# Low parts of the down-projection weights: a negated copy on ScalarE and an adding transfer in place of a subtraction on VectorE

## The chip, the cores and the metric

The kernel runs on one core of one Trainium2 chip. The metric is the device time of one execution in microseconds (us). The kernel before was timed in three runs, and the median stands for it.

## The reference, cut to what matters

One decoder layer on 256 tokens of width 2048, in float32: a mixer (a gated recurrence and a differential attention, side by side), a layer norm, a SwiGLU network, a second layer norm, a gate with a per-layer input, and a third layer norm. The change touches the third product of the SwiGLU network alone, the one with `w_down` (5632 x 2048):

```python
def swiglu(h, w_gate, w_up, w_down):
    g = jnp.einsum('bsd,df->bsf', h, w_gate)
    u = jnp.einsum('bsd,df->bsf', h, w_up)
    return jnp.einsum('bsf,fd->bsd', jax.nn.silu(g) * u, w_down)

h = layer_norm(ALPHA * h + swiglu(h, w_gate, w_up, w_down), ln2_g, ln2_b)
```

## The kernel before, in words

**The split.** Every large product is made from high and low parts: a float32 value is written as hi + lo = w, where hi is the value rounded to the type `fp32r` of the tensor engine and lo is what remains. A product is then three matmuls (hi x hi, hi x lo, lo x hi). The activations are split once per stage; the weights are split as they arrive.

**The weight stream.** All weights are cut into units of 128 x 2048 float32 (1 MB each). The class `Stream` holds them in the order of their use. A unit is loaded on the SyncE queue (SP) into a buffer `w`, of which there are three (line 96). It is then split by halves of 128 x 1024: ScalarE (ACT) writes the high part `wh` (line 114, `prepare_hi`), and VectorE (DVE) subtracts it from the loaded weights and writes the low part `wl` (line 106, `prepare_lo`). There are six buffers for `wh` and six for `wl`, so six halves can be under way.

**The order.** The tensor engine's work is cut into quarters of a unit. After each, `tick()` emits the stages of all other work that are due and then calls `prepare()`: the low part of the half whose high part was emitted last, the loads that have become possible, and the high part of one more half if there is room for it (`room`: at most six halves ahead of those given back). Each engine runs what was emitted for it in that order:

```python
def prepare(self):
    if self.los < self.his:
        self.prepare_lo()
    self.load()
    if self.room():
        self.prepare_hi()
```

**The SwiGLU network.** The hidden width is walked in three parts (`FPARTS`) of 16, 16 and 12 tiles of 128 features. Each part first makes its gate and up products (lines 196 and 197), then its down product: four column blocks of 512, each from 4, 4 or 3 units of `w_down` (16, 16 and 12 units, 44 in all, 88 halves). `token_rows` makes for each row tile and each half of the tokens three matmuls of 512 columns (lines 222 to 224); line 223 is the only one that reads `wl`. A half of a unit is used by 12 such matmuls:

```python
nc.tensor.matmul(ps, ah, wh[:, c], start=first, stop=False)
nc.tensor.matmul(ps, ah, wl[:, c], start=False, stop=False)
nc.tensor.matmul(ps, al, wh[:, c], start=False, stop=last)
```

In the last block of the last part, the last two units are walked twice, for one half of the tokens after the other (`token_halves`), and the second layer norm starts between the two.

**GpSimd (POOL)** issues a few loads of its own (the residual input, norm weights, biases) and does small arithmetic of the norms (lines 621 to 623). It issues nothing while the down products run, up to the norm that ends the third part.

Of the kernel before, what the change touches and what calls it, by code (L numbers as in the profile page):

```python
# [11 lines left out]
F32 = mybir.dt.float32  # L12
# [39 lines left out]
class Stream:  # L52
    """The weight units [128, 2048] in the order of their use, and the work that runs
    beside them. The tensor engine's work is cut into quarters of a unit; after each,
    tick() emits a stage of every job that is due, and then prepares weights: a unit is
    loaded, and split by halves, hi + lo = w exactly, each with at most 12 significant
    bits."""

    def __init__(self, nc, pool, srcs, after_load, pairs):
        self.nc, self.pool, self.srcs, self.after_load = nc, pool, srcs, after_load  # L60
        self.order = [(n, j) for n in range(len(srcs)) for j in range(2)]
        for n in pairs:
            self.order[2 * n:2 * n + 4] = [(n, 0), (n + 1, 0), (n, 1), (n + 1, 1)]
        self.loaded = self.released = self.his = self.los = 0
        self.freed = self.seen = 0
        self.w32, self.parts, self.jobs, self.spare = {}, {}, [], []
        self.unit = 0
        self.held = False
# [35 lines left out]
    def prepare_lo(self):  # L104
        wh, wl = self.parts[self.order[self.los]]
        self.nc.vector.tensor_tensor(wl, self.source(self.los), wh.bitcast(F32), ALU.subtract)  # L106
        self.released += self.order[self.los][1]
        self.los += 1
        self.load()

    def prepare_hi(self):
        src = self.source(self.his)
        wh, wl = self.new_half()
        self.nc.scalar.copy(wh, src)  # L114

# [41 lines left out]
def tile_hybrid_layer(ctx: ExitStack, tc: tile.TileContext, t: dict):  # L157
# [8 lines left out]
    # ---------------------------------------------------------------- the weight units  # L166
# [8 lines left out]
    pair = len(srcs)  # L175
    for f0, nf in FPARTS:
        srcs += [t[n][f0 + i] for i in range(nf) for n in ("w_gate", "w_up")]
        srcs += [t["w_down"][f0 // 4 + kq, blk] for blk in range(4) for kq in range(nf // 4)]
    srcs += [t["w_pg"][blk, kq] for blk in range(4) for kq in range(4)]
    after_load = {}  # L180
    st = Stream(nc, wp, srcs, after_load, [pair])
# [7 lines left out]
    # ---------------------------------------------------------------- products  # L189
    def feature_rows(ps, n, xhl, k0, k1):  # L190
        """ps [128 features, tokens] += unit n's row tiles k0..k1 times x: x_hi W_hi + x_hi W_lo
        in the first half of the bank, x_lo W_hi in the second."""
        for k in range(k0, k1):
            wh, wl = st.half(n, k // 8)
            c = slice((k % 8) * P, (k % 8 + 1) * P)
            nc.tensor.matmul(ps, wh[:, c], xhl[:, k, :], start=(k == 0), stop=False)  # L196
            nc.tensor.matmul(ps[:, :S], wl[:, c], xhl[:, k, :S], start=False, stop=(k == KT - 1))  # L197

    def feature_major(xhl, name, units=1):
        """The next units, row tiles outside."""  # L200
        n = st.take(units)
        pss = [bank(name) for _ in range(units)]
        for q in range(4):
            for u, ps in enumerate(pss):
                feature_rows(ps, n + u, xhl, 4 * q, 4 * q + 4)
                st.free(q % 2)
                st.tick()
        return pss if units > 1 else pss[0]

    def gather(out, ps):  # L210
        """out = the sum of both halves of a feature-major bank, in two stages."""
        nc.scalar.copy(out, ps[:, S:])  # L212
        yield
        nc.vector.tensor_tensor(out, ps[:, :S], out, ALU.add)

    def token_rows(ps, n, ahl, i, k, h, first, last, cols=slice(0, 512)):
        """ps [tokens of half h, columns] += a's row tile k times row tile i of unit n."""
        wh, wl = st.half(n, i // 2)
        c = slice((i % 2) * 512 + cols.start, (i % 2) * 512 + cols.stop)
        ah = ahl[:, k, h * P:(h + 1) * P]  # L220
        al = ahl[:, k, S + h * P:S + (h + 1) * P]
        nc.tensor.matmul(ps, ah, wh[:, c], start=first, stop=False)  # L222
        nc.tensor.matmul(ps, ah, wl[:, c], start=False, stop=False)  # L223
        nc.tensor.matmul(ps, al, wh[:, c], start=False, stop=last)  # L224

    def token_major(ps, ahl, kq, first, last):
        """ps[half] += a's row tiles of quarter kq times the next unit."""
        n = st.take()
        for i in range(4):
            for h in range(2):  # L230
                token_rows(ps[h], n, ahl, i, 4 * kq + i, h, first and i == 0, last and i == 3)
            st.free(i % 2)
            st.tick()

    def token_halves(ps, ahl, kqs, first, last, then=None):
        """The next units, one token half after the other."""
# [14 lines left out]
    # ---------------------------------------------------------------- start  # L251
# [3 lines left out]
    # the tensor engine's clock rises while the first loads are on their way  # L255
# [20 lines left out]
    # x^T, split: [:, k, :256] high parts, [:, k, 256:] low parts; it comes in along  # L276
    # with the first weight units, which take it as it comes
# [44 lines left out]
    # ---------------------------------------------------------------- small values  # L322
# [7 lines left out]
    def small_values():  # L330
        # softplus(-lambda) = max(-lambda, 0) + log1p(e), e = exp(-|lambda|);
        # log1p(e) = 2 atanh(e / (2 + e)) by its series, e / (2 + e) <= 1/3
# [8 lines left out]
        # lambda of the differential attention, on every partition  # L341
# [26 lines left out]
    def relative_bias():  # L368
        # r[h, j] = table[bucket(255 - j), h], masked where 255 - j < 0, on 128 rows
        rps = aux("rps")  # L370
        nc.tensor.matmul(rps[:H, :RW], rb, oh, start=True, stop=True)
        yield
        nc.vector.tensor_copy(rv[:, :S], rps[:H, :S])
        nc.vector.memset(rv[:, S:], NEG)
        nc.gpsimd.dma_start(rd1, rv)
        nc.gpsimd.dma_start(rd, rd1.unsqueeze(1).broadcast_to([H, P, RW]))

    # ---------------------------------------------------------------- RG-LRU
    # 128 channels at a time: convolution and gates
# [40 lines left out]
    def recurrence():  # L420
        # a = exp(-8 gate softplus); with t = tanh(4 gate softplus) = (1 - a) / (1 + a),
        # sqrt(1 - a^2) = (1 + a) sqrt(t)
# [24 lines left out]
    # values, token-major  # L447
# [8 lines left out]
    for blk in range(2):  # L456
        ps = [bank("vps") for _ in range(2)]
        for kq in range(4):
# [3 lines left out]
            if blk == 1 and kq == 0:  # L462
                # bt[p, h, c] = r[h, 127 - p + c] (columns 0..127: the block below the diagonal
                # one, 128..255: the diagonal block): rows of r, read with a pitch one short
# [4 lines left out]
    # ---------------------------------------------------------------- heads  # L469
    mhl = act.tile([P, KT, 2 * S], F32R, tag="A", name="mhl")  # L470

    def lru_out(b, ps):
        """y gelu(yg), split, as row tile b of the merged heads."""
# [25 lines left out]
    def attention(h, qps, kps):  # L499
# [11 lines left out]
        # the two score heads on the diagonal of [2 * 64, 2 * keys]  # L511
# [7 lines left out]
        # scores; softmax_1 - lambda softmax_2 of the head, [queries, keys] by blocks  # L519
# [39 lines left out]
        # times values; RMS norm, [queries, features] by blocks  # L559
# [34 lines left out]
    # ---------------------------------------------------------------- output projection, LN1  # L594
# [22 lines left out]
    def norm_scale(stats, h, n=4):  # L617
        """mean, 1 / deviation, - mean / deviation"""
# [32 lines left out]
    def norm_to(script, xhl, pss, scale, stats, gb, cols):  # L651
        """z <- LN(z); xhl <- z^T, split, in the order of the script: by ticks, the steps of
        token half h and column block b: sh the last residual and the scale, uhb and zhb the
        norm, thb the transposition and high part, lhb the low part; vhb keeps a block of the
        per-layer inputs; H and L prepare weights.
        A block with xhb is scaled before the transposition, thb, takes g and b after it, yhb,
        and rhb does the same for z."""
# [73 lines left out]
    def ple_unit():  # L731
        """Half of the per-layer input projection."""
# [19 lines left out]
    # the projection of the per-layer input runs while the norm is worked out  # L752
# [3 lines left out]
    # ---------------------------------------------------------------- SwiGLU, LN2  # L756
# [41 lines left out]
    # ---------------------------------------------------------------- per-layer gate, LN3  # L798
# [36 lines left out]
    # the last block: the second token half's columns in two pieces, one after the other  # L835
# [47 lines left out]
def _buckets():  # L883
    """T5 bucket of each distance 0..255 (a constant of the shapes)."""
# [18 lines left out]
def _stationary(w):  # L903
    """(2048, F) -> (F/128, 128 rows, 16 row tiles * 128 features)."""
# [4 lines left out]
def _moving(w):  # L909
    """(R, C) -> (C/512, R/512, 128 rows, 4 row tiles * 512 columns)."""  # L910
# [4 lines left out]
def _channels(a):  # L915
    """(..., 1024) -> (128, 8, ...)"""
# [49 lines left out]
```

## Time and profile before

| what | value |
|---|---|
| median of three runs | 1204.46 us (1200.2 to 1206.15) |
| the profiled execution: span from the first to the last instruction | 1199.7 us |
| TensorE busy (PE) | 1182.0 us, 99% of the span |
| VectorE busy (DVE) | 775.7 us, 65% |
| ScalarE busy (ACT) | 607.5 us, 51% |
| GpSimd busy (POOL) | 34.3 us, 3% |
| bytes moved by DMA | 234.83 MB, 196 GB/s over the span |

For the profiled execution only its span is given; what lies around the span is not shown by itself. The median of the runs is 4.8 us longer than that span. Times are in microseconds from the start of the span; MB are millions of bytes, so a unit of "1024.0 KB" is 1.049 MB. Matmuls are pipelined, and one that is shown as 0.39 us long is followed by the next after about 0.23 us.

### The profile page before, as it was taken

Reading aid. Unit: us, or ns where it says so; the run is one execution under the profiler, and the core shown is the slowest. Engines: PE = TensorE matmul, PEld = TensorE weight load, DVE = VectorE, ACT = ScalarE, POOL = GpSimd, SP = SyncE. Lnnn points to the kernel's source line nnn. Section 1 sums busy time; section 2 is a strip of 40 time slices with the busy share of each in tenths; the row PEclk is TensorE's granted clock in tenths of the full one; section 3 lists DMA queues with packets and bytes.
Section 4 is the critical chain, followed back from the end, with each engine's and each line's share of the span. In section 5 each row is a group of like instructions: output and inputs, shape, how many; then the busy total and the mean of one; then the engine's idle time right before and its main releaser. Section 6 shows DMA issues by size and latency. Waiting matters only on the chain.

```text
span 1199.7 us, 15640 instructions
## 1 busy us (share of the span) xinstructions
PE 1182.0 (99%) x6210; PEld 1008.2 (84%) x6210; DVE 775.7 (65%) x1066; ACT 607.5 (51%) x945; POOL 34.3 (3%) x60
## 2 busy tenths in 40 slices
PE   9999999999999999999999999999999999999995
PEld 7888888888888888888888888888888888887885
DVE  6976988785678555564455555554455555556977
ACT  6767576664456454443335444443344454435640
POOL 0000000001010000000000000000000000002001
PEclk9999999999999999999999999999999999999998
DMA  9765454547638555555555555555555555554741
GB/s 332 263 219 196 174 176 148 181 164 287 235 119 315 183 203 177 200 186 197 189 199 187 176 189 196 176 181 205 186 200 176 190 196 175 182 204 150 281 166 70
DMA packets 38872, 234.83 MB, mean 196 GB/s; under 512 B 4432, under 2 KB 8440, under 8 KB 12048
## 3 DMA queue, kind: packets, MB, share of 16 engines
q1 hardware_dynamic: 35952, 221.51, 52.7%
q0 software_dynamic: 2848, 12.34, 2.7%
q8 instruction: 48, 0.79, 0.2%
q14 instruction: 24, 0.20, 0.0%
HBM read 231.72 MB, written 3.68 MB: 196 GB/s over the span
## 4 chain that ended last, share of the span: by engine, by line
PE 94%; DVE 3%; ACT 1%; POOL 1%; DMA 1%; issue 0%; SPq 0%; DVEq 0%; POOLq 0%; ACTq 0%
PE u L196 13%; PE g L196 13%; PE u L197 7%; PE g L197 7%; PE dps L223 7%; PE dps L224 7%; PE dps L222 6%; PE ops L222 2%; PE ops L223 2%; PE ops L224 2%; PE xr L196 2%; PE k L196 2%; PE yg L196 2%; PE q L196 2%; PE gps L223 2%; PE gps L222 2%
## 5 line engine op out<-in xcount | busy, mean ns | idle before, releaser
L106 DVE TENSOR_TENSOR wl<-w,wh 128x1024 fp32r<-128x1024 f32 x404 | 493.0, 1223 | 277.3 <-ACT wh L114 271.3
L114 ACT CAST wh<-w 128x1024 fp32r<-128x1024 f32 x404 | 423.9, 1052 | 309.3 <-PE dps L224 143.7
L196 PE MATMUL u<-x,wh 128*128 128x512 f32 x688 | 243.4, 396 | 0.0
L196 PE MATMUL g<-x,wh 128*128 128x512 f32 x688 | 243.4, 396 | 0.0
L197 PE MATMUL u<-x,wl 128*128 128x256 f32 x688 | 193.0, 281 | 0.0
L197 PE MATMUL g<-x,wl 128*128 128x256 f32 x688 | 193.0, 281 | 0.0
L196 PEld LDWEIGHTS u<-x,wh 128*128 128x128 f32 x688 | 129.1, 188 | 30.8
L196 PEld LDWEIGHTS g<-x,wh 128*128 128x128 f32 x688 | 129.1, 188 | 30.8
L222 PE MATMUL dps<-wh,hT 128*128 128x512 f32 x352 | 137.1, 389 | 0.0
L224 PE MATMUL dps<-wh,hT 128*128 128x512 f32 x352 | 137.0, 389 | 0.0
L223 PE MATMUL dps<-wl,hT 128*128 128x512 f32 x352 | 137.0, 389 | 0.0
L197 PEld LDWEIGHTS g<-x,wl 128*128 128x128 f32 x688 | 130.0, 189 | 0.1
L197 PEld LDWEIGHTS u<-x,wl 128*128 128x128 f32 x688 | 130.0, 189 | 0.0
L222 PEld LDWEIGHTS dps<-wh,hT 128*128 128x128 f32 x352 | 66.1, 188 | 13.8
L223 PEld LDWEIGHTS dps<-wl,hT 128*128 128x128 f32 x352 | 66.1, 188 | 13.6
L224 PEld LDWEIGHTS dps<-wh,hT 128*128 128x128 f32 x352 | 66.1, 188 | 13.6
L212 ACT COPY g<-g 128x256 f32<-128x256 f32 x43 | 16.0, 372 | 79.4 <-PE g L197 79.4
L212 ACT COPY uu<-u 128x256 f32<-128x256 f32 x43 | 16.0, 373 | 77.0 <-PE u L197 77.0
L222 PE MATMUL ops<-wh,mhl 128*128 128x512 f32 x128 | 50.3, 393 | 0.0
L223 PE MATMUL ops<-wl,mhl 128*128 128x512 f32 x128 | 49.9, 390 | 0.0
L224 PE MATMUL ops<-wh,mhl 128*128 128x512 f32 x128 | 49.9, 390 | 0.0
L196 PE MATMUL xr<-xhl,wh 128*128 128x512 f32 x128 | 46.5, 406 | 1.6 <-ACT wh L71 1.5
(227 smaller groups left out, 1598.6 us busy)
## 6 DMA issues: line engine op xcount, KB each, us to landing
w<-in_w_gate SPq DMA_DIRECT2D x44, 1024.0 KB, 4.9
w<-in_w_up SPq DMA_DIRECT2D x44, 1024.0 KB, 4.8
w<-in_w_down SPq DMA_DIRECT2D x44, 1024.0 KB, 4.9
w<-in_w_a SPq DMA_DIRECT2D x28, 1024.0 KB, 4.9
w<-in_w_out SPq DMA_DIRECT2D x16, 1024.0 KB, 4.9
w<-in_w_pg SPq DMA_DIRECT2D x16, 1024.0 KB, 5.0
w<-in_w_v SPq DMA_DIRECT2D x8, 1024.0 KB, 4.9
lng<-in_ln_g POOLq DMA_DIRECT2D x3, 1024.0 KB, 5.9
```

The costliest lines, as they stand in the source:

```text
L106: self.nc.vector.tensor_tensor(wl, self.source(self.los), wh.bitcast(F32), ALU.subtract)
L114: self.nc.scalar.copy(wh, src)
L196: nc.tensor.matmul(ps, wh[:, c], xhl[:, k, :], start=(k == 0), stop=False)
L197: nc.tensor.matmul(ps[:, :S], wl[:, c], xhl[:, k, :S], start=False, stop=(k == KT - 1))
L212: nc.scalar.copy(out, ps[:, S:])
L222: nc.tensor.matmul(ps, ah, wh[:, c], start=first, stop=False)
L223: nc.tensor.matmul(ps, ah, wl[:, c], start=False, stop=False)
L224: nc.tensor.matmul(ps, al, wh[:, c], start=False, stop=last)
```

## The change

For the units of `w_down` alone (their numbers are collected in the set `by_dma`), the subtraction on DVE is left out. In its place ACT, right after the high part, writes the negated high part into `wl`, and a transfer issued on the GpSimd queue reads the same half of the weights from memory a second time and adds it to what stands in `wl`. The unit's load into `w` stays, since the high part is made from it. All other weights keep the old way. (The diff also blanks comments.)

```diff
     def prepare_lo(self):
         wh, wl = self.parts[self.order[self.los]]
-        self.nc.vector.tensor_tensor(wl, self.source(self.los), wh.bitcast(F32), ALU.subtract)
+        if self.order[self.los][0] not in self.by_dma:
+            self.nc.vector.tensor_tensor(wl, self.source(self.los), wh.bitcast(F32), ALU.subtract)
         self.released += self.order[self.los][1]
         self.los += 1
         self.load()

     def prepare_hi(self):
         src = self.source(self.his)
+        n, j = self.order[self.his]
         wh, wl = self.new_half()
         self.nc.scalar.copy(wh, src)
+        if n in self.by_dma:
+            self.nc.scalar.mul(wl, wh.bitcast(F32), -1.0)
+            self.nc.gpsimd.dma_start(wl, self.srcs[n][:, j * 1024:j * 1024 + 1024], accum_op=ALU.add)
...
+    by_dma = set()
     for f0, nf in FPARTS:
         srcs += [t[n][f0 + i] for i in range(nf) for n in ("w_gate", "w_up")]
+        by_dma.update(range(len(srcs), len(srcs) + nf))
         srcs += [t["w_down"][f0 // 4 + kq, blk] for blk in range(4) for kq in range(nf // 4)]
```

## Rows read from the trace of the kernel before

**Rows 1.** The page, busy time of each engine and share of the span.

```profile
span 1199.7 us, 15640 instructions
PE 1182.0 (99%) x6210; PEld 1008.2 (84%) x6210; DVE 775.7 (65%) x1066; ACT 607.5 (51%) x945; POOL 34.3 (3%) x60
```

**Rows 2.** Waits of PE, whole span: total us, times, longest.

```profile
PE tp L681 <- ACT z L675: 1.6, 2, 1.4
PE xr L196 <- ACT wh L71: 1.5, 1, 1.5
PE wps L260 <- DVE zero L257: 1.2, 1, 1.2
PE sps L526 <- DVE khl L517: 0.6, 1, 0.6
```

**Rows 3.** Waits in the first down stage (537 to 626), all engines.

```profile
ACT wh L114 <- PE dps L224: 52.7, 32, 1.7
DVE wl L106 <- ACT wh L114: 42.5, 32, 1.5
```

**Rows 4.** Timeline of PE at the first down stage's start and end (start, length).

```profile
536.99 0.39 PE L222 MATMUL dps<-wh,hT 128*128 128x512 f32 x1
...
623.84 0.39 PE L224 MATMUL dps<-wh,hT 128*128 128x512 f32 x1
624.07 0.39 PE L196 MATMUL g<-x,wh 128*128 128x512 f32 x1
```

**Rows 5.** Timeline of ACT around the first down stage's start (start, length).

```profile
523.25 1.05 ACT L114 CAST wh<-w 128x1024 fp32r<-128x1024 f32 x1 [1.00 <-ACT g L764]
...
537.46 1.05 ACT L114 CAST wh<-w 128x1024 fp32r<-128x1024 f32 x1
...
539.99 1.05 ACT L114 CAST wh<-w 128x1024 fp32r<-128x1024 f32 x1 [1.07 <-PE dps L224]
542.72 1.05 ACT L114 CAST wh<-w 128x1024 fp32r<-128x1024 f32 x1 [1.68 <-PE dps L224]
```

**Rows 6.** The page, costliest groups: both halves of the split (busy, mean ns, idle before).

```profile
L106 DVE TENSOR_TENSOR wl<-w,wh 128x1024 fp32r<-128x1024 f32 x404 | 493.0, 1223 | 277.3 <-ACT wh L114 271.3
L114 ACT CAST wh<-w 128x1024 fp32r<-128x1024 f32 x404 | 423.9, 1052 | 309.3 <-PE dps L224 143.7
```

**Rows 7.** Groups of ACT by form, whole span: scaled and plain passes of one size.

```profile
L764 ACT ACTIVATE g<-g 128x256 f32<-128x256 f32 x44 | 18.5, 420 | 0.4 <-DVE g L214 0.4
L770 ACT CAST hT<-g 128x256 fp32r<-128x256 f32 x44 | 17.9, 407 | 1.0 <-DVE g L768 0.9
L684 ACT CAST x<-tp 128x512 fp32r<-128x512 f32 x10 | 5.8, 588 | 2.6 <-PE tp L681 2.6
L675 ACT ACTIVATE z<-z,mv 128x512 f32<-128x512 f32 x6 | 4.9, 817 | 4.6 <-POOL mv L623 4.6
```

**Rows 8.** Stretches: busy of PE, PEld, DVE, ACT, POOL; clock, DMA share, GB/s.

```profile
523.00:537.00 14.00, 6.51 (x9) 1.00 0.57 187
537.00:626.00 89.00, 89.00 (x397) 73.77 (x396) 45.81 (x44) 35.46 (x35) 0.00 (x0) 1.00 0.56 195
```

(The first of the two was asked for ACT alone.)

**Rows 9.** The same view, two stretches with transfers of both queues under way.

```profile
372.00:380.00 8.00, 8.00 (x49) 7.06 (x48) 4.36 (x6) 5.05 (x8) 0.00 (x0) 1.00 1.01 425
292.00:300.00 8.00, 8.00 (x37) 6.64 (x36) 5.99 (x8) 3.17 (x3) 0.00 (x0) 1.00 1.02 421
```

**Rows 10.** Groups of POOL: issue of its transfers (busy, mean ns, idle before).

```profile
L605 POOL DMA_DIRECT2D z<-in_x x4 | 3.0, 742 | 5.6 <-PE ups L578 5.6
L805 POOL DMA_DIRECT2D pb<-in_b_ple x4 | 2.2, 562 | 23.7 <-DVE pg L812 23.7
```

**Rows 11.** DMA view, 65 to 79: GB/s in 40 slices; issue with KB, us to landing.

```profile
GB/s 140 164 351 398 492 304 328 468 191 247 211 211 212 211 211 211 211 211 211 211 211 234 374 211 328 418 439 376 464 373 347 240 279 328 174 224 402 424 421 398
...
rd<-rd POOLq DMA_DIRECT2D x1, 1536.0 KB, 13.7
```

**Rows 12.** DMA view, 280 to 300: issues, KB each, us to landing.

```profile
w<-in_w_out SPq DMA_DIRECT2D x4, 1024.0 KB, 8.5
z<-in_x POOLq DMA_DIRECT2D x4, 512.0 KB, 8.6
```

**Rows 13.** Timeline of SP around the first down stage (start, from first to last, issues).

```profile
523.21 71.09 SPq L96 DMA_DIRECT2D w<-in_w_down  x14
599.41 0.33 SPq L96 DMA_DIRECT2D w<-in_w_gate  x1
```

**Rows 14.** Stretches in which PE pauses (columns as in the second of rows 8).

```profile
6.00:10.00 4.00, 2.54 (x13) 1.80 (x12) 2.36 (x7) 2.23 (x7) 0.00 (x0) 1.00 0.97 295
1090.00:1095.00 5.00, 3.62 (x20) 2.65 (x19) 2.83 (x4) 2.21 (x4) 3.33 (x4) 1.00 0.10 30
1190.00:1199.70 9.70, 0.00 (x0) 0.00 (x0) 5.60 (x9) 0.00 (x0) 2.44 (x3) 0.50 0.28 108
```

**Rows 15.** The page, bytes read and written in memory.

```profile
HBM read 231.72 MB, written 3.68 MB: 196 GB/s over the span
```

More of the change, by code (lines that the diff above doesn't have):

```diff
@@ L52, with __init__ @@
 class Stream:
-    def __init__(self, nc, pool, srcs, after_load, pairs):
+    def __init__(self, nc, pool, srcs, after_load, pairs, by_dma):
+        self.by_dma = by_dma
         self.nc, self.pool, self.srcs, self.after_load = nc, pool, srcs, after_load
@@ L180, in tile_hybrid_layer @@
     after_load = {}
-    st = Stream(nc, wp, srcs, after_load, [pair])
+    st = Stream(nc, wp, srcs, after_load, [pair], by_dma)
     def bank(name):
```

## The prediction, made before the changed kernel was run

> **What bounds the kernel now.** I read the busy times first, then the waits of PE, then the down stage by itself. PE is busy for 1182.0 of 1199.7 us [rows 1], and its own waits add up to under 5 us, none of them on a low part `wl` [rows 2]. So PE's sequence of matmuls sets the time, and work taken off another engine is worth only what PE waits for it.
>
> In the first down stage the waits run the other way: ACT waits 32 times for PE to give a `wh` buffer back, and DVE 32 times for ACT [rows 3]. Both preparing engines are ahead of PE; the subtraction that the change removes ends early each time. PE walks the 16 units from 536.99 to 624.07 [rows 4], 87.08 us: 5.44 us for a unit, 2.72 us for a half. ACT copies a half every 2.73 us [rows 5], so the whole chain runs in step with PE.
>
> How far ahead is it? The copy at 539.99 was released by the end of the first half's matmuls and fills its buffer for the seventh half (six buffers). The first half's copy is therefore six copies earlier, at 523.25 [rows 5], 13.7 us before PE uses it at 536.99 [rows 4]. That lead is all that a slower way of making `wl` can use up.
>
> **The change, part by part.**
>
> *DVE.* 88 subtractions of 1.223 us go [rows 6]: 108 us of DVE time, 1.2 us out of each 2.72. Gain: nothing, as DVE is ahead [rows 2, 3].
>
> *ACT.* 88 negations are added. A plain pass over 1024 columns takes 1.052 us [rows 6]. A scaled pass was 1.03 times a plain one at 256 columns and 1.39 times at 512 (there with two per-row operands) [rows 7], so 1.05 to 1.46 us. I take 1.06, as the change's scale is a constant. ACT then needs 2.1 us (at most 2.5) of each 2.72; before the stage, where swiglu work runs beside it, it was busy 6.51 of 14 us [rows 8], and five negations make that 11.8. It stays inside: cost nothing, and what hides it is ACT's wait for PE. If a negation took over 1.67 us, ACT would set the pace.
>
> *POOL.* 88 issues are added. An issue took 0.56 to 0.74 us [rows 10], say 0.6 in 2.72, on an engine that does nothing in those stretches (0.00 busy) [rows 8]. Each issue waits there for its negation; queued behind it are only later adding transfers, and at the end the arithmetic of the second norm, which comes after the last of them. Cost nothing.
>
> *SP.* The loads stay, one per 5.44 us (14 from 523.21 over 71.09 us) [rows 13]. They now wait for ACT's copy instead of DVE's subtraction, about a microsecond sooner, with no gain, since no PE wait is on a load.
>
> *DMA.* This is the term that counts. The adding transfers fetch 44 more units, 46.1 MB on top of 231.72 [rows 15], all in three stretches. With two queues at work all engines together moved 421 to 425 GB/s at a share of 1.01 to 1.02 [rows 9]: that is full, and a load of 1.049 MB costs L = 2.47 us of all engines there. [...] The cost A of adding one unit, two transfers of 512 KB, stands in no row. Below, it moves as a plain transfer does: A = 2.47. Above, the slowest stretch of a POOL transfer in this trace is the plateau of 211 GB/s [rows 11]; at that rate, with both the weights and the old content fetched, A = 2 x 1.049 / 0.211 = 9.94. I take A = 2 x 2.47 = 4.94: the nearest row is the full-rate mix of plain transfers of both queues [rows 9], and an addition in place has to fetch two bytes (new and old) for each byte it writes, where those fetched one.
>
> In the Trainium skill, "Collectives: The Full Stack", section "The bandwidth ceiling: the fold count and why AG ≠ RS ≠ AR", a reducing transfer is said to run at about half the rate of a copying one because of its two reads (ratio 1.93). By that page's ratio, an estimate, A would be 4.77 and the sum below 58 us; no row here shows an adding transfer.
>
> *The sum.* A first stage of N = 16 units: the first half's copy starts at 523.25; copy, negation and issue take 2.7 us, so its transfer can start at 526.0, 11.0 us before PE starts the stage. The last half is used 31 x 2.72 = 84.3 us after that start. From first transfer to last use there are thus 95.3 us. In them the engines have 16 additions and, since loads are paced by the copies, about 16 loads: 16 x (2.47 + 4.94) = 118.6 us. The last low part is late by 23.3 us, and so is the end of the stage; lateness doesn't carry on, because the next halves' low parts are made by DVE. The second part is alike: 23.3. In the third (12 units) the last two units are walked by token halves, so the last half is first used after 20 x 2.72 + 3 x 1.36 = 58.5 us: 12 x 7.41 = 88.9 against 69.5, late by 19.4. Sum: 66 us.
>
> *The clock.* PE would be busy about 2.72 of each 3.7 us. With pauses of such a share the granted clock stayed at 1.00, the higher of its levels (2.54 busy of 4.00 us, 3.62 of 5.00); at 0.50 it stands only where PE did nothing [rows 14]. So I add nothing.
>
> The profiled span becomes 1199.7 + 66 = 1265.7. The median of the runs lies 4.8 us above that span; I carry this over: **1270 us**.
>
> **The rivals.**
>
> *Hidden (not slower).* The addition costs little more than a plain transfer. The place is the DMA share in the down stages, and the point that decides is 16 x (L + A) = 95.3, so A = 3.5 us for a unit, 1.4 times a plain one. At A = 2.47 the engines need 4.94 us of each 5.44. From issue to use there are 11 us, and POOL's four transfers of 512 KB issued together beside four loads took 8.6 us to land [rows 12]. For it: the room in the DMA share, 0.56. Against it: the old content must be fetched too. Time: 1204, no change.
>
> *Much slower.* The addition does its fetches and its write one after the other, A = 3 x 2.47 = 7.4: 16 x 9.88 = 158.1, late by 62.8, twice, and 12 x 9.88 - 69.5 = 49.1; sum 175, 1379 us. At the upper bound of 9.94 the same working gives 103.3, 103.3 and 79.4, sum 286, 1490 us. For it: the trace has no in-place addition that shows overlap. Against it: plain transfers of both queues overlapped well enough to fill the engines [rows 9].
>
> *Faster.* DVE's relief would have to reach PE. All PE waits together are 4.9 us [rows 2], below what could be told apart.
>
> The change does do what it says: the numbers put into `by_dma` are those of all 44 units of `w_down`, and nothing else leaves DVE.
>
> **How the numbers follow.** About 0.5% (6 us) is what a measurement of this kernel can tell from no change. Forecast, A from 4.1 to 6.5: 29 to 135 us, 1233 to 1339, chance 0.50. Between the hidden case and the forecast (A of 3.7 to 4.1): 0.05. Much slower, beyond 1339: 0.20. Hidden: 0.22. Faster: 0.03. So slower 0.75, same 0.22, faster 0.03. The range takes in the forecast, the middle case, the part of the hidden case at or above 1203, and the much slower case up to A = 7.4 with some margin: 1203 to 1390.
>
> **What would show it.** Right: in the down stages the DMA share goes to 1.0; PE's waits on `wl` (line 223) appear as the largest group, released by the DMA, and add up to some 66 us in three stretches, growing only after a first stretch of each stage; a pair of adding transfers at full share takes about 5 us; the negation takes 1.05 us; no other wait of PE grows. Wrong: PE waits from the first half of each stage on (then the time to land of one transfer decides, not the rate); a DMA share clearly below 1.0 while PE waits (then the adding queue by itself is slow); PE waits on `wh` (then ACT sets the pace or the loads starve); or no waits at all (hidden). A granted clock below 1.00 in these stages would be a term that I left out.

## The result and the profile after

The changed kernel takes 1296.17 us (three runs, 1292.78 to 1296.79) against 1204.46: 91.7 us more, a ratio of 1.0755 (95% interval 1.072 to 1.0791). The prediction was 1270, slower, by an adding transfer that costs the DMA engines twice a plain one; the range of 1203 to 1390 holds the time, and the loss is 1.4 times the 65.5 us foreseen. The profiled execution has a span of 1293.5 us, 93.8 more than that of before.

The page after, with its busy times and the lines of the 40 slices for PE's clock and the DMA engines, answers to [rows 1]:

```profile
span 1293.5 us, 15852 instructions
PE 1211.3 (94%) x6210; PEld 1010.2 (78%) x6210; DVE 670.1 (52%) x978; ACT 699.2 (54%) x1033; POOL 109.4 (8%) x148
PEclk9999999999999999999999999999999999998998
DMA  9665444557375555899965555799975557995661
```

DVE has lost its 106 us of work and ACT has gained 92, about as computed. The three groups of high digits in the DMA line are the down stages; before, those slices stood at 5. The waits of PE (total us, times, longest), to be set beside [rows 2]:

```profile
PE dps L232 <- DMA wl<-in_w_down: 64.4, 47, 2.4
PE xr L205 <- ACT wh L73: 1.8, 1, 1.8
```

One new wait has come: the matmul that reads `wl` (line 232 now, line 223 before) waits for the adding transfer. Its 64.4 us are less than the loss; the weight load of the same matmul, which comes first and waits for the same thing, shows 90.4 (the page's groups: busy, mean ns, idle before and what ended most of it):

```profile
L232 PEld LDWEIGHTS dps<-wl,hT 128*128 128x128 f32 x352 | 68.2, 194 | 103.2 <-DMA wl<-in_w_down 90.4
```

The stage itself is the best measure. PE's timeline at the first and last matmul of the first down stage, beside [rows 4]:

```profile
539.41 0.40 PE L231 MATMUL dps<-wh,hT 128*128 128x512 f32 x1
...
657.88 0.39 PE L233 MATMUL dps<-wh,hT 128*128 128x512 f32 x1
```

With 0.23 us for the last one, the stage takes 118.7 us instead of 87.1. The same for the second and third stages, of the kernel before and then of the changed one:

```profile
804.96 0.40 PE L222 MATMUL dps<-wh,hT 128*128 128x512 f32 x1
891.84 0.39 PE L224 MATMUL dps<-wh,hT 128*128 128x512 f32 x1
1027.73 0.40 PE L222 MATMUL dps<-wh,hT 128*128 128x512 f32 x1
1095.49 0.39 PE L224 MATMUL dps<-wh,hT 128*128 128x512 f32 x1
```

```profile
838.99 0.40 PE L231 MATMUL dps<-wh,hT 128*128 128x512 f32 x1
957.32 0.39 PE L233 MATMUL dps<-wh,hT 128*128 128x512 f32 x1
1093.21 0.40 PE L231 MATMUL dps<-wh,hT 128*128 128x512 f32 x1
1189.28 0.39 PE L233 MATMUL dps<-wh,hT 128*128 128x512 f32 x1
```

The second takes 118.6 instead of 87.1 and the third 96.3 instead of 68.0. The three are longer by 31.6, 31.5 and 28.3 us, 91.4 together, out of the 93.8 by which the span grew. So nearly all of the loss lies here. The stretches view (busy times of PE, PEld, DVE, ACT, POOL, then PE's clock, DMA share, GB/s) shows who is full, before the stage and inside it, beside [rows 8]:

```profile
525.00:539.00 14.00, 14.00 (x81) 12.12 (x81) 1.99 (x5) 11.68 (x14) 3.49 (x4) 1.00 0.88 234
560.00:620.00 60.00, 48.35 (x201) 36.26 (x200) 2.73 (x4) 35.34 (x34) 13.63 (x16) 1.00 1.05 279
```

No engine is busy all the time any more; the DMA engines are, at a share of 1.05. At 279 GB/s a load and its addition, 2.097 MB counted once each, take 7.52 us for a unit; the prediction had 7.41. The DMA issues (KB each, median us to landing):

```profile
w<-in_w_down SPq DMA_DIRECT2D x44, 1024.0 KB, 9.0
wl<-in_w_down POOLq DMA_DIRECT2D x88, 512.0 KB, 17.1
```

An adding transfer lands 17.1 us after its issue, longer than the 11 us that the lead leaves. Is that its own time, or a queue? The experiments had to tell.

### The profile page after: what moved, and what is told of

Same layout as the page of the kernel before. It is cut to its first block, busy times and chain, and to the rows that moved or that the text cites. A ratio compares the mean times of both kernels' runs of the same rounds, so it can differ in the third digit from the quotient of the medians.

```text
span 1293.5 us, 15852 instructions
## 1 busy us (share of the span) xinstructions
PE 1211.3 (94%) x6210; PEld 1010.2 (78%) x6210; DVE 670.1 (52%) x978; ACT 699.2 (54%) x1033; POOL 109.4 (8%) x148
## 4 chain that ended last, share of the span: by engine, by line
PE 72%; DMA 20%; DVE 3%; issue 2%; ACT 1%; POOL 1%; SPq 0%; DVEq 0%; POOLq 0%; ACTq 0%
DMA wl<-in_w_down 20%; PE g L205 12%; PE u L205 12%; PE g L206 6%; PE u L206 6%; PE ops L232 2%; PE ops L233 2%; PE ops L231 2%; PE xr L205 2%; PE k L205 2%; PE yg L205 2%; PE dps L232 2%; PE q L205 2%; PE gps L232 2%; PE gps L231 2%
## 5 line engine op out<-in xcount | busy, mean ns | idle before, releaser
L109 DVE TENSOR_TENSOR wl<-w,wh 128x1024 fp32r<-128x1024 f32 x316 | 385.2, 1223 | 209.6 <-ACT wh L118 203.3
L232 PE MATMUL dps<-wl,hT 128*128 128x512 f32 x352 | 148.4, 422 | 64.9 <-DMA wl<-in_w_down 64.4
L232 PEld LDWEIGHTS dps<-wl,hT 128*128 128x128 f32 x352 | 68.2, 194 | 103.2 <-DMA wl<-in_w_down 90.4
L233 PE MATMUL dps<-wh,hT 128*128 128x512 f32 x352 | 141.8, 403 | 0.0
L231 PE MATMUL dps<-wh,hT 128*128 128x512 f32 x352 | 141.3, 401 | 0.0
L121 POOL DMA_DIRECT2D wl<-in_w_down x88 | 75.0, 852 | 719.9 <-ACT wl L120 680.3
L120 ACT ACTIVATE wl<-wh 128x1024 fp32r<-128x1024 f32 x88 | 93.2, 1059 | 2.8
L651 DVE TENSOR_TENSOR z<-z,dps 128x512 f32<-128x512 f32 x16 | 10.9, 684 | 152.1 <-PE dps L233 152.1
L231 PEld LDWEIGHTS dps<-wh,hT 128*128 128x128 f32 x352 | 68.6, 195 | 15.8
L233 PEld LDWEIGHTS dps<-wh,hT 128*128 128x128 f32 x352 | 68.7, 195 | 12.6
L223 DVE TENSOR_TENSOR uu<-u,uu 128x256 f32<-128x256 f32 x43 | 18.2, 424 | 61.9 <-ACT uu L221 61.9
## 6 DMA issues: line engine op xcount, KB each, us to landing
wl<-in_w_down POOLq DMA_DIRECT2D x88, 512.0 KB, 17.1
```

The lines of the kernel that those rows point to most:

```text
L120: self.nc.scalar.mul(wl, wh.bitcast(F32), -1.0)
L121: self.nc.gpsimd.dma_start(wl, self.srcs[n][:, j * 1024:j * 1024 + 1024], accum_op=ALU.add)
L651: nc.vector.tensor_tensor(z[:, h, c], z[:, h, c], ps, ALU.add)
```

## The experiments

**Theory:** the sixteen DMA engines are shared and full; an addition costs them two fetches, and PE waits for the sum of loads and additions. **Rivals:** reading the weights twice exhausts memory; the GpSimd queue, or one transfer's own landing time, sets the pace; the adder itself is slow.

### A plain transfer in the same place

```diff
-            self.nc.gpsimd.dma_start(wl, self.srcs[n][:, j * 1024:j * 1024 + 1024], accum_op=ALU.add)
+            self.nc.gpsimd.dma_start(wl, self.srcs[n][:, j * 1024:j * 1024 + 1024])
```

> The transfer writes the weights plainly into the low part instead of adding them to it: the same bytes from memory, the same queue, sizes and waits, but nothing has to be fetched from the destination (the low parts then hold the whole weights). Theory (the sixteen DMA engines are shared and full; an addition costs them twice a plain transfer, 5.0 us for a unit beside 2.5 for its load): the engines need 4.95 us of each 5.44, the stages are as long as before, 1204 to 1212 us, and PE waits for the transfer for under 5 us in all. Rival (memory gives no more than it gave, because each weight is read twice): as the changed kernel, about 1296. Rival (the GpSimd queue or its issue is slow, whatever the transfer does): about 1296, with a time to land near 17 us.

Measured: 1204.68 us, ratio 1.0001 (0.9987 to 1.0014). The stretch 560 to 620, and the transfer's line of the DMA issues:

```profile
560.00:620.00 60.00, 60.00 (x266) 49.67 (x265) 6.83 (x8) 43.08 (x41) 10.04 (x19) 1.00 1.02 374
```

```profile
wl<-in_w_down POOLq DMA_DIRECT2D x88, 512.0 KB, 7.0
```

The same bytes come from memory at 374 GB/s, PE is busy throughout, and a transfer lands in 7.0 us. This one run settles five terms at once. Taken together, the negation on ACT, the 88 issues on POOL, the moved wait of SP, the second read of the weights and the missing work of DVE cost and gain nothing. Only the addition is left.

### Fewer additions: half and three quarters

```diff
-        if n in self.by_dma:
+        if n in self.by_dma and not j:
```

(The subtraction in `prepare_lo` comes back for the other halves.)

> Only the first half of each unit of the down weights is made by the adding transfer, the second half by the subtraction on VectorE as before. Theory (shared, full engines): 2.5 + 2.5 = 5.0 us of each 5.44: hidden, 1204 to 1212 us. Rival (one adding transfer takes longer to land than its lead, whatever else runs): PE still waits at every adding half, some 45 us in all, 1245 to 1255.

And three quarters:

```diff
-        if n in self.by_dma:
+        if n in self.by_dma and not (j and n % 2):
```

> Three halves of four are made by the adding transfer. Theory (shared, full engines): 2.5 + 3.75 = 6.2 us for a unit against 5.44 of PE; 99 us of work for a stage of 16 units that takes 87, less what of the lead is left: 20 to 40 us in all, 1224 to 1244. Rival (the adding queue is a limit by itself, one transfer per 3.75 us, and the loads don't count): 24 transfers need 90 us, the lead covers it: 1204 to 1210.

Measured: half, 1204.91 us, ratio 1.0006 (0.9989 to 1.0023); three quarters, 1239.95 us, ratio 1.0287 (1.0259 to 1.0314), 35 us more. PE's wait for the transfer in the second:

```profile
PE dps L232 <- DMA wl<-in_w_down: 21.8, 16, 2.0
```

The knee lies where loads and additions together pass PE's 5.44 us for a unit, as the theory has it. A limit of the adding queue alone would have hidden three quarters.

### The transfers by themselves

Behind the end of the kernel before, five groups of twelve transfers on the GpSimd queue, with nothing else under way (one execution, for its trace):

```diff
+    for i in range(12):
+        nc.gpsimd.dma_start(dst[i % 6], t["w_gate"][i][:, 0:1024])
+    for i in range(12):
+        nc.gpsimd.dma_start(dst[i % 6], t["w_gate"][i][:, 0:1024], accum_op=ALU.add)
+    for i in range(12):
+        nc.gpsimd.dma_start(dst[i % 6], own[i % 6].bitcast(F32))
+    for i in range(12):
+        nc.gpsimd.dma_start(dst[i % 6], own[i % 6].bitcast(F32), accum_op=ALU.add)
+    for i in range(12):
+        nc.gpsimd.dma_start(dst[i % 6].bitcast(BF16), own[i % 6].bitcast(BF16), accum_op=ALU.add)
```

> The kernel before, with five groups of twelve transfers of 512 KB on the GpSimd queue behind its end, into six low-part buffers that nothing else uses: plain from memory, adding from memory, plain from another buffer on the chip, adding from another buffer on the chip, and the last again with the bytes taken as 16-bit numbers, so twice as many additions. The span grows by their sum; only the rates count. Theory (an addition costs the engines a second fetch, wherever the operands lie): 420, 210, 420, 210 and 210 GB/s of bytes written. Rival (the adder is slow by the element): the adding groups as they may be, but the 16-bit group at half the rate of the 32-bit one. Rival (memory is the limit): adding on the chip clearly faster than adding from memory.

Stretches from the middle of each group, in the same order (the last two columns are DMA share and GB/s):

```profile
1210.00:1216.00 6.00, 0.00 (x0) 0.00 (x0) 0.00 (x0) 0.00 (x0) 2.74 (x5) 0.50 1.13 417
1225.00:1237.00 12.00, 0.00 (x0) 0.00 (x0) 0.00 (x0) 0.00 (x0) 3.81 (x6) 0.50 1.06 210
1252.00:1261.00 9.00, 0.00 (x0) 0.00 (x0) 0.00 (x0) 0.00 (x0) 3.97 (x8) 0.50 1.15 415
1270.00:1279.00 9.00, 0.00 (x0) 0.00 (x0) 0.00 (x0) 0.00 (x0) 2.72 (x4) 0.50 1.06 209
1300.00:1318.00 18.00, 0.00 (x0) 0.00 (x0) 0.00 (x0) 0.00 (x0) 5.07 (x6) 0.50 1.06 199
```

Plain 417, adding 210: a factor of 1.99, with a full share in each case. The operands' place doesn't matter (415 and 209 on the chip), so memory is not the limit. Twice the number of additions in the same bytes costs 5% (199 against 209), not a factor of two, so an adder that is slow by the element isn't either. What halves the rate goes by bytes. The second fetch is the reading that I keep, as it fits all five; an adder slow by the byte would fit them too, and no run tells the two apart. The price is the same for both: A = 1.049 / 0.210 = 4.99 us, where the prediction took 4.94.

### Additions without the loads

```diff
+                if n in self.by_dma:
+                    self.nc.vector.memset(w, 0.5)
+                    continue
                 self.nc.sync.dma_start(w[:, c], self.srcs[n][:, c])
```

> The load of the down weights into their buffer is left out; VectorE fills the buffer with a constant (so high parts are made from a constant, and low parts are the weights less that constant). The 88 adding transfers stay as they are. Theory (shared, full engines): without the loads the engines need 5.0 us for a unit against 5.44: hidden or nearly so, 1204 to 1215 us, though the additions still take twice a plain transfer. Rival (the adding queue is a limit by itself at 3.75 us a transfer, 7.5 us a unit): as the changed kernel, 1285 to 1300.

Measured: 1223.76 us, ratio 1.0163 (1.0123 to 1.0203). The rival falls, but the theory's upper bound of 1215 is missed by 9 us. A stretch in the middle of the first stage, and all the matmuls of that stage for which PE's timeline shows a wait for the transfer:

```profile
570.00:595.00 25.00, 25.00 (x112) 20.70 (x111) 10.13 (x7) 19.57 (x19) 8.17 (x10) 1.00 1.05 193
```

```profile
618.44 0.50 PE L235 MATMUL dps<-wl,hT 128*128 128x512 f32 x1 [1.74 <-DMA wl<-in_w_down]
622.17 0.50 PE L235 MATMUL dps<-wl,hT 128*128 128x512 f32 x1 [0.70 <-DMA wl<-in_w_down]
625.87 0.50 PE L235 MATMUL dps<-wl,hT 128*128 128x512 f32 x1 [0.67 <-DMA wl<-in_w_down]
```

In the middle PE never pauses (25.00 of 25.00), though additions alone hold the engines at 1.05. All waits fall in the last 10 us of the stage. What is new there? The DMA view of 600 to 628 lists four loads of the next stage beside the last additions, which now take 13.3 us to land instead of the run's 5.8:

```profile
wl<-in_w_down POOLq DMA_DIRECT2D x5, 512.0 KB, 13.3
w<-in_w_up SPq DMA_DIRECT2D x2, 1024.0 KB, 9.2
w<-in_w_gate SPq DMA_DIRECT2D x2, 1024.0 KB, 7.7
```

That pointed at the term that the prediction had mis-sized: the number of loads that compete with a stage's additions.

### Without the next stage's first loads

```diff
+                if n not in self.by_dma and any(n - i in self.by_dma for i in (1, 2, 3)):
+                    self.nc.vector.memset(w, 0.5)
+                    continue
                 self.nc.sync.dma_start(w[:, c], self.srcs[n][:, c])
```

> As the changed kernel, but the three units behind each group of down weights (gate and up weights, or the last gate's) are not loaded: VectorE fills their buffers with a constant. Theory (the prediction counted too few loads beside a stage's additions: the next stage's first loads run while the last additions are queued): nine loads fewer at 2.47 us each, 22 us less than the changed kernel: 1268 to 1280. Rival (the missing time lies in the start of each stage, where the engines aren't full yet, or in the lowered clock of PE): 1290 to 1298, as the changed kernel.

Measured: 1268.43 us, ratio 1.0532 (1.05 to 1.0564), 27.7 us less than the changed kernel (the kernel before, timed beside this run, took 1201.78). PE's timeline, first and last matmul of the first stage:

```profile
540.61 0.40 PE L234 MATMUL dps<-wh,hT 128*128 128x512 f32 x1
...
650.60 0.39 PE L236 MATMUL dps<-wh,hT 128*128 128x512 f32 x1
```

110.2 us: late by 23.1, where the prediction worked out 23.3 from 16 loads. The second and third stages are late by 23.3 (predicted 23.3) and 17.1 (19.4). The rival falls. But fewer than 16 loads ran beside a stage's additions here, so part of this agreement is luck; the section on the prediction works it out.

And with both sets of loads left out:

```diff
+                if any(n - i in self.by_dma for i in range(4)):
+                    self.nc.vector.memset(w, 0.5)
+                    continue
                 self.nc.sync.dma_start(w[:, c], self.srcs[n][:, c])
```

> As the run without the loads of the down weights, and the three units behind each group aren't loaded either (constants in their place). Theory (the 19 us that remained there come from the next stage's loads beside the last additions): nothing but additions runs in the down stages, 5.0 us of each 5.44: 1204 to 1210 us, PE waits for them under 3 us. Rival (additions alone are still too slow for PE, or a transfer's own landing time counts at the end of a stage): 1214 to 1224, as without the loads alone.

Measured: 1202.93 us, ratio 0.9995 (0.9978 to 1.0013). PE's wait for the transfer in the whole run:

```profile
PE dps L235 <- DMA wl<-in_w_down: 0.2, 1, 0.2
```

So the 19 us go with the next stage's loads.

### How many are under way

Two runs asked whether 17 us are a transfer's own time. The first limits the order written down by the stream to four halves ahead:

```diff
-        return self.his < min(self.seen + 2 * BUFS + spare, len(self.order)) and self.order[self.his][0] < self.loaded
+        lead = 4 if self.his < len(self.order) and self.order[self.his][0] in self.by_dma else 2 * BUFS
+        return self.his < min(self.seen + lead + spare, len(self.order)) and self.order[self.his][0] < self.loaded
```

> For the down weights only four halves may be under way instead of six; else as the changed kernel. Theory (shared, full engines; a transfer takes 17 us to land because it queues behind others): the engines stay full with four under way, each stage loses at most the two halves of lead, 5.4 us: 1296 to 1315 us, and a transfer now lands in about 10 us. Rival (the 17 us are a transfer's own time, and six under way set the pace): the round of landing, copy, negation and use, 22.5 us, is shared by four instead of six, 5.6 us a half instead of 3.75: about 1296 + 88 x 1.9 = 1460.

Measured: 1308.0 us, ratio 1.0872 (1.0835 to 1.0909), as the theory's range had it; but a transfer still landed in 17.2 us, not 10, so the run didn't do what it was meant to. Inside a stage nothing on ACT stands between the copies, and ACT runs on into all six buffers whatever was written after what. Only the start moved, where the copies stand behind other work of ACT: each stage is 4.5 to 4.9 us longer (123.5, 123.0 and 101.2), and in the first the first transfer is issued 6.8 us before PE starts the stage (529.38 and 536.19) instead of 11.5. That is a price for lead, not an answer to the question.

The second takes buffers away:

```diff
-            wl = self.pool.tile([P, 1024], F32R, tag="wl", name="wl", bufs=2 * BUFS)
+            if self.order[i][0] in self.by_dma or i % 6 < 4:
+                wl = self.pool.tile([P, 1024], F32R, tag="wl", name="wl", bufs=4)
+            else:
+                wl = self.pool.tile([P, 1024], F32R, tag="wx", name="wl", bufs=2)
```

> The changed kernel with four low-part buffers for the down weights instead of six, so that at most four adding transfers are really under way (other weights keep six). Theory (shared, full engines; landing times are queueing): the engines stay full; each stage loses about two halves of lead, 1300 to 1318 us, and a transfer lands in 9 to 13 us. Rival (17 us are a transfer's own time): the round of landing, copy, negation and use is shared by four, about 5.6 us a half: 1400 to 1470, with the DMA share well below 1.0 in the stages.

Measured: 1293.03 us, ratio 1.0724 (1.0693 to 1.0756). The transfer's line of the DMA issues, and the stretch 560 to 620:

```profile
wl<-in_w_down POOLq DMA_DIRECT2D x88, 512.0 KB, 10.9
```

```profile
560.00:620.00 60.00, 47.41 (x190) 34.20 (x189) 2.74 (x4) 31.91 (x32) 13.64 (x16) 1.00 1.05 278
```

With four under way a transfer lands in 10.9 us, the share stays at 1.05, the rate at 278 GB/s. So the 17 us were queueing. The time came out below what I expected (no loss at all, where I had put two halves of lead a stage). By stages it is 117.1, 116.8 and 100.6 us, against 118.7, 118.6 and 96.3. The trace shows that the first stage lost no lead: its first transfer is issued at 525.50, 11.3 us before PE starts at 536.79. From there to the last landing at 650.96, the DMA view gives for the loads' queue (packets, MB, share of 16 engines):

```profile
q1 hardware_dynamic: 2417, 17.57, 35.7%
```

In the changed kernel it is 18.71 MB (shown below). So 1.1 loads fewer ran beside these additions, 2.7 us at 2.47 each, and this time from the first issue to the last landing is 2.1 us shorter. In the third stage, the longer one, PE waits 3.7 us for the second norm behind the last transfer, where it waited 0.6 in the changed kernel; the cause of that stays open.

No run beat the kernel before, and none was to be expected: in it PE waits for nothing that these parts change.

## Why the prediction was right, and where its size was off

**The bound.** PE set the time before, DVE's relief brought nothing, and the loss comes from the DMA engines in the three down stages: as predicted, and shown by the plain transfer (1204.68) against the adding one (1296.17). The 4.8 us carried over from the span to the median were 2.7 here.

**ACT, POOL, SP.** A negation took 1.059 us (1.06 taken). The groups of ACT and POOL (busy, mean ns, idle before):

```profile
L121 POOL DMA_DIRECT2D wl<-in_w_down x88 | 75.0, 852 | 719.9 <-ACT wl L120 680.3
...
L120 ACT ACTIVATE wl<-wh 128x1024 fp32r<-128x1024 f32 x88 | 93.2, 1059 | 2.8
```

An issue took 0.85 us, over the 0.6 taken; with the plain transfer in its place it was 0.53. It stays hidden: POOL is busy for 13.63 of 60 us. The first stage's first transfer was issued at 527.86, 11.5 us before the stage began; the prediction had 11.0.

**The cost of an addition.** 4.94 was taken, 4.99 measured alone. The bounds of 2.47 and 9.94 were wide, and the choice by counting fetched bytes held. The Trainium skill, "Collectives: The Full Stack", section "The bandwidth ceiling: the fold count and why AG ≠ RS ≠ AR", puts the halved rate of a reducing transfer between cores down to its second read, not to the adder, with a measured ratio of 1.93. The trace agrees with the ratio, 1.99 between plain and adding transfers, and with an adder that costs little by the element, 5% between 16-bit and 32-bit additions; the second read itself no run shows.

**The step that was mis-sized** is "about 16 loads" in the sum. SP's timeline (start, extent, issues) shows what runs beside the first stage's additions, issued from 527.86 on, the last landing at 655:

```profile
525.32 89.34 SPq L98 DMA_DIRECT2D w<-in_w_down  x14
621.85 0.33 SPq L98 DMA_DIRECT2D w<-in_w_gate  x1
629.38 0.33 SPq L98 DMA_DIRECT2D w<-in_w_up  x1
636.86 0.33 SPq L98 DMA_DIRECT2D w<-in_w_gate  x1
645.61 0.33 SPq L98 DMA_DIRECT2D w<-in_w_up  x1
653.16 0.33 SPq L98 DMA_DIRECT2D w<-in_w_gate  x1
```

The prediction stopped counting loads at the last copy of a down weight. But the last adding transfers then still stand 17 us deep in the queue, and PE goes on giving buffers back, so the next stage's loads are issued and take their share beside them. On the other side, the first loads of this stage are over before its additions begin. From the first addition's issue to the last one's landing, 527.86 to 655.41, the DMA view gives for the loads' queue:

```profile
q1 hardware_dynamic: 2572, 18.71, 37.2%
```

These are 17.8 units of 1.049 MB, not 16. In the terms of the sum, this time was to be 118.6 us and is 127.6, against 95.8 from first issue to last use (11.5 + 84.3; 95.3 in the prediction): late by 31.7, and the stage lost 31.6. Of the 8.9 us more, 1.84 loads at 2.47 make 4.5 and the dearer addition 0.8. For the 3.6 that remain no run shows the cause.

In the run without the next stage's first loads the same view, from 529.06 to 646.29, gives:

```profile
q1 hardware_dynamic: 2038, 14.86, 32.0%
```

These are 14.2 units. Lateness falls to 23.1, 23.3 and 17.1 us, 63.5 in all; with those loads it is 91.4. Over the three stages the loads moved 40.6 MB beside the additions instead of 51.7, which is 10.7 units, 26.3 us at 2.47, of the 27.9 saved. So the next stage's loads cost what their bytes cost. The sum itself was short by 25.4 us in the three stages: the loads as they ran (49.3 units instead of 44) make 13.2 of them and the dearer addition 2.2; some 10 us stay open. That 63.5 lies so near to the sum's 66.0 is partly luck: with the 14.2 loads that really ran, and 4.99 for an addition, the sum would give 19 us for the first stage, not the 23.1 measured.

**The clock** was put at no cost because short pauses before had left it at 1.00 [rows 14]. In the changed kernel the granted clock did fall to its lower level (0.50, 1.2 of 2.4 GHz), six times in the three stages: five times for about 3.4 us, and at the end of the third stage for nearly 7. In the 4.00 us before each fall PE had been busy for 1.98 to 2.23 us, where the shorter stretch of [rows 14] at full clock has 2.54 of 4.00. The prediction had spread PE's pauses evenly, 2.72 busy of each 3.7 us; the waits came in bunches. The first fall and the last:

```profile
552.00:556.00 4.00, 2.02 (x8) 1.39 (x7) 0.00 (x0) 2.10 (x2) 0.55 (x1) 0.91 1.05 278
556.00:560.00 4.00, 4.00 (x13) 3.18 (x13) 0.00 (x0) 0.38 (x1) 0.31 (x1) 0.67 1.04 274
...
1176.00:1180.00 4.00, 1.58 (x5) 1.00 (x4) 0.00 (x0) 0.00 (x0) 0.00 (x0) 0.56 0.43 126
1180.00:1184.00 4.00, 4.00 (x12) 3.18 (x11) 2.34 (x4) 0.18 (x1) 0.63 (x1) 0.59 0.00 0
```

Inside a stage the DMA engines stay full meanwhile (1.04 to 1.05), so PE gives up time that it would have waited. The first stage bears out that this cost nothing there: the engines' share is 1.04 from the first addition's issue to the last one's landing at 655.41, and PE's last matmul starts at 657.88, 2.5 us behind it, the time of eleven matmuls at 0.23 us. The last fall, at the end of the third stage, has no transfer left to hide behind: some ten matmuls stand 0.43 us apart instead of 0.23, about 2 us, and a shorter wait for the norm behind them (0.6 us instead of 1.4) gives part of that back.

**The rivals.** "Hidden" was the right picture of a plain transfer, not of an adding one; its deciding point, an addition of 3.5 us, lies between the two measured costs. "Much slower" had fetches and write one after the other, which 210 GB/s excludes (that way would give 142). The changed profile's signs came as listed, but for the clock. That PE's waits add up to 64.4 us where "some 66" was foreseen is luck: the loss was 91.4, and the waits of PE's weight load, 90.4, come nearer to it.

## What to carry to other kernels

Here an adding transfer cost the DMA engines twice what a plain one costs; before moving a subtraction from an idle engine to them, add up loads and twice the additions against the time of the bound engine in that stage alone, not against the mean share of the span. Count the loads that really run beside the additions, from the first issue to the last landing: what is prefetched for the next stage belongs to them, and what has landed before does not. A long time to land says little by itself: that it was a queue showed when fewer transfers were under way, as it fell from 17.1 to 10.9 us at the same rate (279 and 278 GB/s).

## What the runs showed that was not expected

An adding transfer took POOL 0.85 us to issue, a plain one of the same size in its place 0.53. The DMA share alone can't tell near-full from late: with plain transfers it stood at 1.02 and with additions alone at 1.05 while PE never paused; only with loads and additions together, at the same 1.05, did PE wait. And the granted clock fell although PE's longest wait in these stages was 2.4 us.
